# The last row of the first load in a softmax with relative-position bias, loaded by 16 transfers over fewer and fewer partitions

## The chip, the core and the metric

The kernel runs on one core of a Trainium2 chip. The metric is the device time of one execution in microseconds (us). Runs of one kernel on the same chip are compared, with an interval where there are several rounds. The profile is that of one execution; its span runs from the first to the last instruction of the program, and the execution's own time is a little longer than its span.

## What is computed

The inputs are `logits` of shape (2, 8, 2112, 2112) and `rel_bias` of shape (8, 33), both float32. Each head h adds `rel_bias[h, clip(i - j, -16, 16) + 16]` to the logit of query i and key j, and a softmax is taken along the keys:

```
rel = pos[:, None] - pos[None, :]
rel_clipped = np.clip(rel, -max_rel, max_rel) + max_rel
bias = rel_bias[:, rel_clipped].copy()
logits = logits + bias[None, :, :, :]
logits = logits - logits.max(axis=-1, keepdims=True)
exp = np.exp(logits)
return (exp / exp.sum(axis=-1, keepdims=True)).astype(np.float32)
```

Every logit is read once and every result written once: 285.5 MB each way.

## The kernel before

A row is the 2112 logits of one query, 8448 bytes. The 2112 queries of a head are split into 64 blocks of 33 consecutive rows, and the 128 partitions hold the blocks of two heads: partition p has block p mod 64 of head 2k or 2k + 1. The outer index k (4 values, `K`) goes over pairs of heads. For one k there are 12 chunks (`NT`): two batches, and for each the 33 rows of a block in portions of 6, 5, 6, 5, 6 and 5 rows (`SIZES`, L35). So a chunk is 128 partitions times 5 or 6 consecutive rows, and in one transfer each partition moves one contiguous run of 42,240 or 50,688 bytes. There are 48 chunks in all, and 4 buffers `X[0]` to `X[3]` (L44), used in turn.

Four instruction streams work side by side:

- **SyncE (SP)** issues every load and store of chunks, on one queue. `load(k, m)` (L86) brings chunk m into buffer m mod 4 and raises the semaphore `ld` of that buffer by 16. `store(k, m)` (L90) waits until the chunk's rows are scaled, and writes them out. The start (L100) issues the loads of chunks 0 to 3 at once. Then store 0 is issued (L220), and from there `turn` (L214) goes on by a fixed order: store n, wait until store n-1 has landed, load n+3. The last chunk is stored in two parts, three rows and two.
- **VectorE (DVE)** builds, once per k, a strip `F` of biases of width 2144 (`strip`, L143), a shifted window of which is the bias of any row. For each chunk, `add` (L169) takes the buffer's `ld` semaphore and then, row by row, adds the bias and finds the row's extreme (L173). `scale` (L186) takes the sums of the exponentials, forms reciprocals (L189) and scales the first three rows (L193).
- **ScalarE (ACT)** computes the exponentials with their sums (`exps`, L178, L181) and scales the other two or three rows (`scale_rest`, L195, L198). At the start it also issues the small transfer of `rel_bias` over 4 partitions (L107).
- **GpSimd (POOL)** only makes two small index tables at the start (L112). TensorE does nothing.

The order in which the DMA engines see the work of SyncE's queue is thus: load 0, load 1, load 2, load 3, store 0, store 1, load 4, store 2, load 5, and so on. A wait of SyncE for a semaphore is `take` (L82): wait for a count, then subtract it.

The loop of VectorE over k (L202 to L206) calls `strip(k)` and then `add` and `scale` for its 12 chunks; the first chunk of the first k is the one that the change touches.

Of the kernel before, what the change touches and what calls it, by code (L numbers as in the profile page):

```python
# [15 lines left out]
def kernel(  # L16
# [6 lines left out]
    nc = tc.nc  # L23
    P = 128
    B, H, S, S2 = logits.shape
    assert S == S2
    MR = 16
    W = 2 * MR + 1
# [5 lines left out]
    NBUF = 4  # L34
    SIZES = [6, 5, 6, 5, 6, 5]  # L35
# [8 lines left out]
    X = [io.tile([P, R * S], FP32, tag=f"X{b}", name=f"X{b}") for b in range(NBUF)]  # L44
# [11 lines left out]
    def view(t, offset, dims):  # L56
        return bass.AP(tensor=t.tensor, offset=t.offset + offset, ap=[[list(t.ap[0])[0], P]] + dims)

    def rows(t, k, m, s0, n):

        b, j, r = CH[m]
        return bass.AP(
            tensor=t.tensor,
            offset=t.offset + (b * H * S + j + s0) * S + k * (2 * S * S),
            ap=[[W * S, P], [1, n * S]],
        )

    with tc.tile_critical(no_gpsimd_drain=True):  # L68
        ld = [nc.alloc_semaphore(f"ld{b}") for b in range(NBUF)]
        st = [nc.alloc_semaphore(f"st{b}") for b in range(NBUF)]  # L70
        added = nc.alloc_semaphore("added")
        expd = nc.alloc_semaphore("expd")
# [13 lines left out]
        def load(k, m):  # L86
            b, r = m % NBUF, CH[m][2]
            nc.sync.dma_start(out=X[b][:, 0 : r * S], in_=rows(logits, k, m, 0, r)).then_inc(ld[b], 16)
# [8 lines left out]
                out=rows(out, k, m, s0, n), in_=X[b][:, s0 * S : (s0 + n) * S]  # L97
            ).then_inc(st[b], 16)

        for m in range(NBUF):  # L100
            load(0, m)

        Q = 32
        step = list(F.ap[0])[0]
# [3 lines left out]
            out=bass.AP(tensor=F.tensor, offset=F.offset, ap=[[Q * step, P // Q], [1, H * W]]),  # L108
            in_=bass.AP(tensor=rel_bias.tensor, offset=rel_bias.offset, ap=[[0, P // Q], [1, H * W]]),
# [7 lines left out]
        v = nc.vector  # L117
        done = [0]

        def then(ins):  # L120
            done[0] += 1
            ins.then_inc(dve, 1)

        def settle():
            take(v, dve, done[0])
            done[0] = 0
# [9 lines left out]
        for h in range(2):  # L136
            p = slice(h * NB, (h + 1) * NB)
            src = bass.AP(tensor=F.tensor, offset=F[p].offset + h * W,
                          ap=[[list(F.ap[0])[0], NB], [2 * W, K], [1, W]])
# [3 lines left out]
        def strip(k):  # L143

            then(v.tensor_copy(out=rbK[:, :], in_=rbP[:, bass.ds(k, 1), :]))  # L145
            settle()
            low, high = rbK[:, W - 1 : W], rbK[:, 0:1]
            blocks = view(F, MR, [[W, NB], [1, W]])
            then(v.tensor_tensor(out=blocks, in0=view(eq, 0, [[1, NB], [0, W]]),  # L149
                                 in1=view(rbK, W - 1, [[0, NB], [-1, W]]), op=ALU.mult))  # L150
            then(v.tensor_scalar(out=rest, in0=lt, scalar1=low, scalar2=None, op0=ALU.mult))  # L151
            then(v.tensor_copy(out=F[:, 0:MR], in_=low.to_broadcast([P, MR])))  # L152
            then(v.tensor_copy(out=F[:, FW - MR : FW], in_=high.to_broadcast([P, MR])))  # L153
            settle()
            then(v.scalar_tensor_tensor(out=rest, in0=gt, scalar=high, in1=rest, op0=ALU.mult, op1=ALU.add))  # L155
            settle()
            then(v.tensor_tensor(out=blocks, in0=blocks, in1=view(rest, 0, [[1, NB], [0, W]]), op=ALU.add))  # L157
            settle()
# [10 lines left out]
        def add(m):  # L169
            take(v, ld[m % NBUF], 16)  # L170
            j, r = CH[m][1:]
            for i in range(r):
                v.tensor_tensor_reduce(  # L173
                    out=row(m, i), in0=row(m, i), in1=F[:, W - 1 - j - i : W - 1 - j - i + S],
                    scale=-1.0, scalar=BIG, op0=ALU.add, op1=ALU.min, accum_out=col(nmax, m, i),
                ).then_inc(added, 1)
# [9 lines left out]
        def scale(m):  # L186
            r = CH[m][2]
            take(v, expd, r)
            v.reciprocal(out=col(rec, m, 0, r), in_=col(tot, m, 0, r)).then_inc(inv, 1)  # L189
            v.wait_ge(inv, 1).then_inc(inv, -1)  # L190
            v.sem_inc(invA, 1)
            for i in range(DV):
                v.tensor_scalar_mul(out=row(m, i), in0=row(m, i), scalar1=col(rec, m, i)).then_inc(scaled, 1)  # L193
# [7 lines left out]

        with nc.Fori(0, K, 1, engines=[ENG.DVE]) as k:  # L202
            strip(k)
            for m in range(NT):
                add(m)
                scale(m)  # L206
# [54 lines left out]
```

## Time and profile before

| | us |
|---|---|
| median of 3 runs | 1329.67 |
| lowest and highest | 1329.32, 1330.35 |
| the profiled execution | 1329.3 |
| its span | 1327.5 |
| VectorE busy | 819.7 |
| ScalarE busy | 808.8 |

The page of the profile gives first the busy time of each engine and its share of the span; then the span in 40 equal slices, with the mean busy share of the 16 DMA engines in tenths and the GB/s that they moved; then the DMA queues, where q1 is SyncE's and q10 ScalarE's. "Packets" are the pieces that DMA engines moved. A row of the windows view gives a stretch of the span from A to B, its length, the busy time of each compute engine with the number of its instructions, the clock granted to TensorE, the DMA share and the GB/s, where a packet counts in full in the stretch in which it starts. A row of the timeline gives start, length, engine, line, operation, what is written and read, the form, and in brackets the idle time before and what ended it; "SPq" is SyncE's sequencer. A row of a source line gives durations in ns as min/median/max.

### The profile page before, as it was taken

Reading aid. Unit: us, or ns where it says so; the run is one execution under the profiler, and the core shown is the slowest. Engines: PE = TensorE matmul, PEld = TensorE weight load, DVE = VectorE, ACT = ScalarE, POOL = GpSimd, SP = SyncE. Lnnn points to the kernel's source line nnn. Section 1 sums busy time; section 2 is a strip of 40 time slices with the busy share of each in tenths; the row PEclk is TensorE's granted clock in tenths of the full one; section 3 lists DMA queues with packets and bytes.
Section 4 is the critical chain, followed back from the end, with each engine's and each line's share of the span. In section 5 each row is a group of like instructions: output and inputs, shape, how many; then the busy total and the mean of one; then the engine's idle time right before and its main releaser. Section 6 shows DMA issues by size and latency. Waiting matters only on the chain. (4 is left out here: it accounts for less than half of the span.)

```text
span 1327.5 us, 2383 instructions
## 1 busy us (share of the span) xinstructions
DVE 819.7 (62%) x756; ACT 808.8 (61%) x652; POOL 0.6 (0%) x6
## 2 busy tenths in 40 slices
DVE  6875665558655566556866466664686547665572
ACT  3885575655756557555676566764667646675472
POOL 0000000000000000000000000000000000000000
DMA  9999999999999999999999999999999999999998
GB/s 407 427 424 425 430 433 429 432 431 433 434 430 438 423 439 431 432 432 433 438 436 429 433 430 435 433 430 441 427 439 428 435 431 437 434 436 427 436 427 376
DMA packets 13981, 571.00 MB, mean 430 GB/s; under 512 B 1556, under 2 KB 1560, under 8 KB 1560
## 3 DMA queue, kind: packets, MB, share of 16 engines
q1 hardware_dynamic: 13968, 570.96, 99.8%
q14 instruction: 5, 0.04, 0.0%
q10 hardware_dynamic: 8, 0.00, 0.0%
HBM read 285.48 MB, written 285.47 MB: 430 GB/s over the span
## 5 line engine op out<-in xcount | busy, mean ns | idle before, releaser
L173 DVE CUSTOM_DVE_ANT_0 X<-X,F 128x2112 f32<-128x2112 f32 x264 | 605.5, 2354 | 346.8 <-DVEq L83 346.8
L181 ACT ACTIVATE X<-X,nmax 128x2112 f32<-128x2112 f32 x264 | 542.2, 2054 | 411.5 <-ACTq L83 385.7
L198 ACT ACTIVATE X<-X,rec 128x2112 f32<-128x2112 f32 x120 | 238.7, 2046 | 29.0 <-ACTq L83 29.0
L193 DVE TENSOR_SCALAR X<-X,rec 128x2112 f32<-128x2112 f32 x144 | 181.4, 1316 | 11.6 <-DVEq L190 11.6
L189 DVE RECIPROCAL rec<-tot 128x6 f32<-128x6 f32 (+1 forms) x48 | 9.1, 190 | 116.1 <-DVEq L83 116.1
L181 ACT ACTIVATION_READ_ACCUMULATOR X<-X,nmax 128x1 f32 x264 | 49.3, 187 | 0.0
L181 ACT ACT_TABLE_LOAD x4 | 5.1, 1283 | 55.8 <-ACTq L83 55.8
L173 DVE DVE_READ_ACCUMULATOR2_ANT nmax<- 128x1 f32 x264 | 21.7, 82 | 0.0
L157 DVE TENSOR_TENSOR F<-F,rest 128x2112 f32<-128x2112 f32 x4 | 9.4, 2358 | 0.6
L149 DVE TENSOR_TENSOR F<-Z,rbK 128x2112 f32<-128x2112 f32 x4 | 9.4, 2358 | 0.6
L134 DVE LOAD_MASK_SELECT F<-F x1 | 0.0, 14 | 7.1 <-DMA F<-in_rel_bias_dram 7.1
L155 DVE SCALAR_TENSOR_TENSOR rest<-Z,rbK,rest 128x64 f32<-128x64 f32 x4 | 1.1, 284 | 0.6 <-DVEq L83 0.2
L151 DVE TENSOR_SCALAR rest<-Z,rbK 128x64 f32<-128x64 f32 x4 | 1.1, 275 | 0.0
L105 DVE MEMSET F<- 128x264 f32 x1 | 0.3, 278 | 1.1 <-SPq L68 1.1
L145 DVE COPY rbK<-rbP 128x33 f32 x4 | 0.7, 178 | 0.3 <-DVEq L83 0.3
L153 DVE COPY F<-rbK 128x16 f32<-128x16 f32 x4 | 0.7, 168 | 0.0
L152 DVE COPY F<-rbK 128x16 f32<-128x16 f32 x4 | 0.7, 166 | 0.0
L132 DVE TENSOR_SCALAR Z<-F 128x64 f32<-128x64 f32 x3 | 0.5, 223 | 0.1
L140 DVE COPY rbP<-F 64x132 f32<-64x132 f32 x2 | 0.4, 224 | 0.2
L134 DVE STREAM_SHUFFLE F<-F 128x264 f32<-128x264 f32 x1 | 0.4, 443 | 0.0
L112 POOL IOTA F<- 64x64 f32 x2 | 0.4, 179 | 0.7 <-PEq L256 0.6
L245 POOL MEMSET const-bfloat16-1.0<- 128x1 bf16 x1 | 0.1, 103 | 0.0
(3 smaller groups left out, 0.3 us busy)
## 6 DMA issues: line engine op xcount, KB each, us to landing
X<-in_logits_dram SPq DMA_DIRECT2D x24, 6336.0 KB, 39.7
out_dram<-X SPq DMA_DIRECT2D x24, 6336.0 KB, 46.9
X<-in_logits_dram SPq DMA_DIRECT2D x24, 5280.0 KB, 42.2
out_dram<-X SPq DMA_DIRECT2D x23, 5280.0 KB, 48.6
out_dram<-X SPq DMA_DIRECT2D x1, 3168.0 KB, 16.5
out_dram<-X SPq DMA_DIRECT2D x1, 2112.0 KB, 21.1
F<-in_rel_bias_dram ACTq DMA_DIRECT2D x1, 4.1 KB
```

The costliest lines, as they stand in the source:

```text
L145: then(v.tensor_copy(out=rbK[:, :], in_=rbP[:, bass.ds(k, 1), :]))
L149: then(v.tensor_tensor(out=blocks, in0=view(eq, 0, [[1, NB], [0, W]]), in1=view(rbK, W - 1, [[0, NB], [-1, W]]), op=ALU.mult))
L151: then(v.tensor_scalar(out=rest, in0=lt, scalar1=low, scalar2=None, op0=ALU.mult))
L152: then(v.tensor_copy(out=F[:, 0:MR], in_=low.to_broadcast([P, MR])))
L153: then(v.tensor_copy(out=F[:, FW - MR : FW], in_=high.to_broadcast([P, MR])))
L155: then(v.scalar_tensor_tensor(out=rest, in0=gt, scalar=high, in1=rest, op0=ALU.mult, op1=ALU.add))
L157: then(v.tensor_tensor(out=blocks, in0=blocks, in1=view(rest, 0, [[1, NB], [0, W]]), op=ALU.add))
L173: v.tensor_tensor_reduce(out=row(m, i), in0=row(m, i), in1=F[:, W - 1 - j - i : W - 1 - j - i + S], scale=-1.0, scalar=BIG, op0=ALU.add, o ...
L181: nc.scalar.activation(out=row(m, i), in_=row(m, i), func=ACTF.Exp, scale=-1.0, bias=col(nmax, m, i), accum_out=col(tot, m, i),).then_inc( ...
L189: v.reciprocal(out=col(rec, m, 0, r), in_=col(tot, m, 0, r)).then_inc(inv, 1)
L193: v.tensor_scalar_mul(out=row(m, i), in0=row(m, i), scalar1=col(rec, m, i)).then_inc(scaled, 1)
L198: nc.scalar.activation(out=row(m, i), in_=row(m, i), func=ACTF.Copy, scale=col(rec, m, i),).then_inc(scaledA, 1)
```

## The change

The first load, of 6 rows on 128 partitions, is split. Its first 5 rows (`r0`) are loaded by one transfer as before, with the semaphore `ld[0]`. The sixth row of the 128 partitions is loaded by 16 transfers, issued by SyncE between this one and load 1, with a semaphore of their own, `lr`. The first eight, g = 0 to 7, take the partitions g, g + 8, g + 16, ..., over 15 - g partitions. The last eight, g = 7 down to 0, take what is left of each such group, the upper g + 1 partitions. So the numbers of partitions are 15, 14, 13, 12, 11, 10, 9, 8 and then 8, 7, 6, 5, 4, 3, 2, 1: together 128. VectorE waits for `lr` to reach 256, 16 transfers of 16, between `strip(k)` and the first `add`, in each of the four turns of its loop; nothing lowers `lr`, so the wait passes at once after the first turn. Loads 1 to 3 follow in SyncE's queue.

```diff
         ld = [nc.alloc_semaphore(f"ld{b}") for b in range(NBUF)]
+        lr = nc.alloc_semaphore("lr")
...
-        for m in range(NBUF):
+        G = 8
+        N0 = P // G
+        r0 = SIZES[0] - 1
+        nc.sync.dma_start(out=X[0][:, 0 : r0 * S], in_=rows(logits, 0, 0, 0, r0)).then_inc(ld[0], 16)
+
+        def last_row(g, i0, n):
+            p0 = g + G * i0
+            x, d = X[0], rows(logits, 0, 0, r0, 1)
+            step = list(x.ap[0])[0]
+            nc.sync.dma_start(
+                out=bass.AP(tensor=x.tensor, offset=x.offset + p0 * step + r0 * S, ap=[[G * step, n], [1, S]]),
+                in_=bass.AP(tensor=d.tensor, offset=d.offset + p0 * W * S, ap=[[G * W * S, n], [1, S]]),
+            ).then_inc(lr, 16)
+
+        for g in range(G):
+            last_row(g, 0, N0 - 1 - g)
+        for g in reversed(range(G)):
+            last_row(g, N0 - 1 - g, g + 1)
+        for m in range(1, NBUF):
             load(0, m)
...
             strip(k)
+            v.wait_ge(lr, 2 * G * 16)
             for m in range(NT):
```

## The prediction

> **What bounds the kernel.** I read the page first, from its top: who is busy, and in which slices.
>
> ```profile
> span 1327.5 us, 2383 instructions
> DVE 819.7 (62%) x756; ACT 808.8 (61%) x652; POOL 0.6 (0%) x6
> DMA  9999999999999999999999999999999999999998
> DMA packets 13981, 571.00 MB, mean 430 GB/s; under 512 B 1556, under 2 KB 1560, under 8 KB 1560
> q1 hardware_dynamic: 13968, 570.96, 99.8%
> q10 hardware_dynamic: 8, 0.00, 0.0%
> ```
>
> SyncE's queue, q1, occupies the 16 DMA engines for 99.8% of the span, from the second slice to the last but one, while VectorE and ScalarE are idle 38% of it. So the time is the bytes over the rate, plus what an engine loses at the ends and in between. The bytes don't change here; only rate and ends can.
>
> The same lines tell how a transfer is dealt out. There are 97 transfers of 128 partitions (48 loads, 49 stores) and one of 4 partitions, rel_bias on q10. The packets under 512 B are 1556 = 97 x 16 + 4, and q10 has 8 packets, 4 of them data: each engine that takes part adds one small closing packet, a full transfer runs on 16 engines, and the one of 4 partitions ran on 4. So I expect a transfer of n rows on n below 16 partitions to run on n engines, one row each.
>
> Next the rate in stretches of 100 us; the last two columns are the DMA share and GB/s.
>
> ```profile
> core 0: us, DVE busy (x) ACT busy (x) POOL busy (x), PEclk, DMA share, GB/s
> 0.00:100.00 100.00, 73.29 (x75) 67.90 (x55) 0.56 (x6) 1.00 1.00 421
> 100.00:200.00 100.00, 62.40 (x56) 61.52 (x51) 0.00 (x0) 1.00 0.99 427
> 200.00:300.00 100.00, 56.52 (x51) 58.04 (x46) 0.00 (x0) 1.00 1.00 432
> 300.00:400.00 100.00, 68.67 (x66) 64.20 (x54) 0.00 (x0) 1.00 1.00 432
> 400.00:500.00 100.00, 59.05 (x53) 58.18 (x46) 0.00 (x0) 1.00 1.01 434
> ...
> 700.00:800.00 100.00, 59.12 (x54) 58.10 (x48) 0.00 (x0) 1.00 1.00 430
> 800.00:900.00 100.00, 59.29 (x54) 62.82 (x50) 0.00 (x0) 1.00 1.00 434
> ...
> 1200.00:1300.00 100.00, 62.40 (x56) 62.74 (x51) 0.00 (x0) 1.00 1.00 430
> ```
>
> There is a flat ceiling of 434 GB/s, 27.1 per engine, and the rate climbs to it over 400 us: the engines are busy throughout, but their packets last longer at first. Against 434, the first four stretches lose 13, 7, 2 and 2 GB/s, which is 3.0 + 1.6 + 0.5 + 0.5 = 5.6 us. Of that 2.0 us is the start, as the next rows show.
>
> ```profile
> 0.00:2.00 2.00, 0.76 (x4) 0.00 (x0) 0.56 (x6) 1.00 0.26 76
> 2.00:4.00 2.00, 0.00 (x0) 0.00 (x0) 0.00 (x0) 1.00 1.08 329
> ```
>
> Packets start only toward 2 us, and the first of them run at 329: (1 - 329/434) x 2, so 0.5 us and somewhat more, say 0.9 us, is ramp. That leaves **2.7 us of early loss**. The other two slow stretches lose 0.9 us each. Then the end, us by us.
>
> ```profile
> 1321.00:1322.00 1.00, 0.00 (x0) 0.00 (x0) 0.00 (x0) 1.00 0.87 372
> 1322.00:1323.00 1.00, 0.00 (x0) 0.00 (x0) 0.00 (x0) 1.00 0.75 321
> 1323.00:1324.00 1.00, 0.00 (x0) 0.00 (x0) 0.00 (x0) 1.00 0.47 203
> 1324.00:1325.00 1.00, 0.00 (x0) 0.00 (x0) 0.00 (x0) 1.00 0.28 118
> 1325.00:1326.00 1.00, 0.00 (x0) 0.00 (x0) 0.00 (x0) 1.00 0.12 51
> 1326.00:1327.50 1.50, 0.00 (x0) 0.00 (x0) 0.00 (x0) 1.00 0.00 0
> ```
>
> All engines have the same bytes, yet they finish over some 4 us. From 1322 on 321 + 203 + 118 + 51 = 693 KB are left, which 16 engines together would move in 693/434 = 1.6 us: the mean engine ends near 1323.6, the last near 1326.0. **The last engine is 2.4 us behind the mean.** Then 1.5 us to the end of the span, and 1.8 us outside it: 1329.3 for this execution. The median of the runs, 1329.67, is 0.4 above; I work in the former and add 0.4 at the end.
>
> My reading of both: the engines start side by side, and all change from load to store at once; packets there are slow. The delays differ by engine and push them apart; once they are some 4 us apart the rate stays at 434. The change sets them apart from the start.
>
> **The change part by part.**
>
> Bytes and packets: 128 rows of 8448 B leave the first load and return as 16 transfers. One row at an engine's rate is 8448 B / 27.1 GB/s = 0.31 us. The first load was 6 x 8 rows an engine and becomes 5 x 8. If a transfer over n partitions always uses the same first n engines, the first engine gets a row from each of the 16 transfers, the next from 15, and so on; the eighth 9, the ninth 7, the last none. The mean stays 8. The spread is 16 x 0.31 = 5.0 us, and the first engine has 8 x 0.31 = 2.5 us more than the mean. Nothing returns that: the queue never runs dry, so **the engine that is made late is late at the end.** Of the closing packets there are 128 more, 16 on the first engine; their price lies inside the 0.31 per row up to a few ns (bounds 0 and 0.1 us in all).
>
> Issue: SyncE must issue 17 transfers where it issued one before load 1.
>
> ```profile
> L88 SPq DMA_DIRECT2D X<-in_logits_dram x48: 339/349/512, 1.0 to 1244.0; - x48
> L107 ACTq DMA_DIRECT2D F<-in_rel_bias_dram x1: 1098/1098/1098, 1.4 to 1.4; - x1
> 0.97 1.88 SPq L88 DMA_DIRECT2D X<-in_logits_dram  x4
> ```
>
> The first four issues took 1.88 us, 0.47 each; the one issue over few partitions, on another engine's queue, took 1.10. Bounds for 16: 5.6 (0.35 each) to 17.6 us; I take 0.47, by SyncE's own rows: 7.5 us, and load 1 goes out at 1.0 + 0.5 + 7.5 = 9.0. What hides it is the five-row load: 40 x 0.31 = 12.4 us from about 2 us plus 0.9 of ramp, until 15.3. At 1.10 each load 1 is issued at 19.1 and the early engines stand idle for some 4 us; the first engine does not, as its own rows last beyond 20.3.
>
> The new wait: VectorE waits for all 16 transfers ahead of the first row, and what is queued behind it is every row pass, and behind these ScalarE and store 0.
>
> ```profile
> 18.60 2.36 DVE L173 CUSTOM_DVE_ANT_0 X<-X,F 128x2112 f32<-128x2112 f32 x1 [2.15 <-DVEq L83]
> 41.38 16.61 SPq L96 DMA_DIRECT2D out_dram<-X  x2
> ```
>
> Row pass one starts at 18.60 now. With the last row landing between 20.3 and 28 it slips by up to 10 us, and store 0 from 41.4 to at most 52. Loads 1 to 3 (16 rows x 8 x 0.31 = 39.7 us) hold the earliest engine until 15.3 + 39.7 = 55. So it costs nothing; without that cover, early engines would lose their lead, and the late one nothing. In later rounds the count is already reached, and the wait is free.
>
> Stalls: of the 2.7 us of early loss I take 2.0 away (bounds: 0, if standing apart is not the cause, and 4.5, if the two slow stretches go too). The old lag of 2.4 us goes as well, because the planned order takes its place.
>
> The price of a row is the open term. [...] I take 0.62 for the first eight and 0.78, the middle, for the last eight: 5.0 + 6.2 = 11.2 us, because the rate that repeats in loads and stores points to the side that both pass. Against the old 2.5 that is **+8.7**.
>
> [...]
>
> Sum: -2.4 (old lag) - 2.0 (early loss) + 8.7 = +4.3 on 1329.3, so 1333.6, and on the median's scale **1334.0**.
>
> **The rivals.**
>
> Rows at full speed: the first engine's rows take 5.0, +2.5. Then -2.4 - 2.0 + 2.5 = -1.9, 1327.8 on the median's scale; with all 2.7 and the slow stretches gone, down to 1325.3; I take 1327.0. [...]
>
> Standing apart doesn't cure the early loss (or slow issues undo it), at full-speed rows: -2.4 + 2.5 = +0.1, plus the chance lag of up to 2.4 on the first engine: 1329.8 to 1332.2, or slower yet if the late engine stalls more than the mean. For it: a stretch at 430 comes back at 700 and at 1200 us, long after the engines parted.
>
> It doesn't do what it says: short transfers start on changing engines, so that each gets about 8 rows. Then the lag and early loss stay: 1329.7 to 1330. The counts above say how many engines take part, not which. [...]
>
> The forecast ends on the slower side and the first rival on the other; what decides is the first engine's time for 16 rows. At 6.9 us the time is that of before.
>
> **How the numbers follow.** About 0.2%, 2.7 us, is what a measurement tells from no change: under 1327.0 is faster, over 1332.3 slower. Forecast 0.45 (own range 1332 to 1336: slower 0.41, same 0.04). Rows at full speed 0.36 (faster 0.22, same 0.14). No cure 0.13 (same 0.06, slower 0.07). Even deal 0.06 (same). Together 0.22, 0.30, 0.48. The range of 8 in 10 reaches from the full-speed rival, 1326.0, to 1335.8, short of three-way sharing with no cure.
>
> **What would show it.** Packets under 512 B: 1556 + 128 = 1684 if n rows take n engines. The rate in the first 400 us near 434 if the cure holds. At the end, a tail that starts earlier and lasts 10 us or more with sharing, about 5 without. VectorE's first row pass at 26 to 28 us with sharing, near 21 without. Load 1's issue at 9.0. The sum fails if the late engine is not the first one, if the queue runs dry, or if it falls further behind at every change from load to store.

## The result, and the profile after

The changed kernel takes **1334.24 us**, the median of 7 runs (1334.00 to 1334.51); the kernel before takes 1329.63 beside it. The ratio is 1.0035, with a 95% interval of 1.0023 to 1.0047: slower by some 4.6 us. The profiled execution took 1334.34 with a span of 1332.6 us.

The page of the changed kernel, the lines that answer to those shown of before:

```profile
span 1332.6 us, 2399 instructions
DVE 819.7 (62%) x756; ACT 808.8 (61%) x652; POOL 0.6 (0%) x6
DMA  9999999999999999999999999999999999999997
DMA packets 14237, 571.00 MB, mean 428 GB/s; under 512 B 1684, under 2 KB 1688, under 8 KB 1688
q1 hardware_dynamic: 14224, 570.96, 99.5%
```

The busy times and the bytes are those of before, and the small packets are the 1684 that were forecast: a transfer over n partitions ran on n engines. Then the rate in stretches, the last column being GB/s:

```profile
0.00:100.00 100.00, 69.51 (x72) 63.89 (x53) 0.56 (x6) 1.00 0.99 400
100.00:200.00 100.00, 63.41 (x56) 62.37 (x49) 0.00 (x0) 1.00 1.00 434
200.00:300.00 100.00, 57.67 (x54) 61.20 (x50) 0.00 (x0) 1.00 1.00 433
300.00:400.00 100.00, 67.96 (x64) 61.95 (x52) 0.00 (x0) 1.00 1.00 434
...
700.00:800.00 100.00, 58.67 (x53) 57.71 (x45) 0.00 (x0) 1.00 1.00 432
...
1200.00:1300.00 100.00, 59.38 (x53) 58.12 (x47) 0.00 (x0) 1.00 1.00 433
```

Two things changed in opposite directions. From 100 us on the kernel is better than before, which had 427, 432 and 432 in the next three stretches and 430 at 700 and 1200 us. The first 100 us are far worse, 400 in place of 421. Where, the finer stretches show:

```profile
4.00:15.00 11.00, 6.04 (x11) 0.00 (x0) 0.00 (x0) 1.00 1.00 430
15.00:16.00 1.00, 0.38 (x1) 0.00 (x0) 0.00 (x0) 1.00 0.74 254
16.00:18.00 2.00, 0.00 (x0) 0.00 (x0) 0.00 (x0) 1.00 1.24 262
18.00:20.00 2.00, 0.00 (x0) 0.00 (x0) 0.00 (x0) 1.00 1.40 275
20.00:22.00 2.00, 0.00 (x0) 0.00 (x0) 0.00 (x0) 1.00 1.11 194
22.00:24.00 2.00, 0.00 (x0) 0.00 (x0) 0.00 (x0) 1.00 0.96 211
24.00:26.00 2.00, 0.00 (x0) 0.00 (x0) 0.00 (x0) 1.00 0.65 211
26.00:28.00 2.00, 1.01 (x1) 0.00 (x0) 0.00 (x0) 1.00 1.08 465
```

From 15 to 26 us, while the 16 narrow transfers run, the engines have packets under way (the share is 0.65 to 1.40) and move 194 to 275 GB/s, about half of the 430 of the stretch before. From 15 to 28 us they moved 254 + 2 x (262 + 275 + 194 + 211 + 211 + 465) = 3490 KB, which at 434 would take 8.0 us and not 13: by these rows 5.0 us lost on the mean engine.

Two things about such sums. A packet counts in full where it starts, and 16 packets of 50,688 bytes that start together are 0.81 MB. So while the engines stand side by side, the edge of a stretch of 100 us can move its rate by up to 8 GB/s. The trace also keeps every packet of the DMA engines with start, duration and size, but without its engine; numbers from there are marked "by the packet records". With the bytes of each packet spread over its duration, and against 433.8 GB/s, the most that any stretch of 100 us reached so, the loss from 15 to 28 us is **5.5 us on the mean engine**: 2.2 in the narrow rows, 3.1 in the first packets of load 1, the rest in closing packets. Within one engine a packet starts 3 or 4 ns before its predecessor ends: where one is alone at the end, packets of 629 ns start 625 or 626 apart. So the packets can mostly be strung into 16 chains, one for each engine. In the kernels with a staircase the engines are numbered here by the narrow rows in their chains, the first having most.

The timeline has the issues and the end of the rows:

```profile
1.40 11.78 SPq L110 DMA_DIRECT2D X<-in_logits_dram  x16
13.23 1.30 SPq L89 DMA_DIRECT2D X<-in_logits_dram  x3
26.99 2.36 DVE L192 CUSTOM_DVE_ANT_0 X<-X,F 128x2112 f32<-128x2112 f32 x1 [11.61 <-DVEq L84]
```

And the end:

```profile
1322.00:1324.00 2.00, 0.00 (x0) 0.00 (x0) 0.00 (x0) 1.00 0.89 380
1324.00:1326.00 2.00, 0.00 (x0) 0.00 (x0) 0.00 (x0) 1.00 0.53 228
1326.00:1328.00 2.00, 0.00 (x0) 0.00 (x0) 0.00 (x0) 1.00 0.18 76
1328.00:1330.00 2.00, 0.00 (x0) 0.00 (x0) 0.00 (x0) 1.00 0.06 25
1330.00:1332.60 2.60, 0.00 (x0) 0.00 (x0) 0.00 (x0) 1.00 0.02 6
```

An engine moves 42,240 bytes in 1.561 us, 27 GB/s, so after 1328, at 25 GB/s, a single engine is still at work. The packet records put the end of the last engine at 1331.0, of the one before it at 1327.9 and of the mean engine at 1325.6. Before, these were 1326.1, 1325.8 and 1323.8.

### The profile page after: what moved, and what is told of

The parts are those of the page before. It is cut to its first block, busy times and chain, and to the rows that moved or that the text cites. A ratio compares the mean times of both kernels' runs of the same rounds, so it can differ in the third digit from the quotient of the medians.

```text
span 1332.6 us, 2399 instructions
## 1 busy us (share of the span) xinstructions
DVE 819.7 (62%) x756; ACT 808.8 (61%) x652; POOL 0.6 (0%) x6
## 2 busy tenths in 40 slices
DMA packets 14237, 571.00 MB, mean 428 GB/s; under 512 B 1684, under 2 KB 1688, under 8 KB 1688
```

## The experiments

The theory, called S, is that engines which write certain sets of partitions at the same time hold one another up, and that this is what the narrow transfers cost. It is called sharing below; the runs can show its price for a set, not how it comes about. Its rivals: O, small transfers with their closing packets are slow by themselves; H, reading HBM at rows 8 blocks apart is slow. Beside this stand two questions of the prediction: does standing apart cure the early loss, and is an engine that is made late at the start late at the end? All ratios are against the kernel before, run beside. Edits are shown against the kernel before unless the text says otherwise, and `...` marks lines left out; VectorE's wait for `lr` is for 16 times the number of narrow transfers each time. "Rows" are packets of one row, 8448 bytes; their times are from the packet records, as are the ends of engines.

**The row as one transfer.** By none of the three theories should this cost anything. Each experiment of the first kind has the five-row load of the changed kernel and brings the sixth row by other transfers. Here `last_row` takes the first partition, the step between partitions and their number; the next kernels differ from this one only in the calls shown.

```diff
-        for m in range(NBUF):
+        r0 = SIZES[0] - 1
+        nc.sync.dma_start(out=X[0][:, 0 : r0 * S], in_=rows(logits, 0, 0, 0, r0)).then_inc(ld[0], 16)
+
+        def last_row(p0, d, n):
...
+                out=bass.AP(tensor=x.tensor, offset=x.offset + p0 * step + r0 * S, ap=[[d * step, n], [1, S]]),
+                in_=bass.AP(tensor=t.tensor, offset=t.offset + p0 * W * S, ap=[[d * W * S, n], [1, S]]),
...
+        last_row(0, 1, P)
+        for m in range(1, NBUF):
             load(0, m)
```

> [...] Rival O (rows in small pieces are slow by themselves, because of the closing packets or short packets): one closing packet for eight rows, so no loss either. Rival H (the slow thing is reading HBM at rows 8 blocks apart): no loss. This is the control.

Measured: 1329.83, ratio 1.0001 (0.9991 to 1.0011); all 128 packets of 8448 B took 0.319 us. Splitting the load off costs nothing.

**Sixteen partitions, 8 apart.**

```diff
+        for g in range(8):
+            last_row(g, 8, 16)
```

> The last row by eight transfers over 16 partitions that lie 8 apart: every engine gets eight rows with eight closing packets, none is made late. Theory S: two engines meet everywhere, a row takes 0.62 us, every engine loses 8 x 0.31 = 2.5 us, time about 2.5 us above before, 1332. Rivals O and H: rows of 0.62 us as well, the same time. Between 16 and 26 us the changed kernel moved 194 to 275 GB/s; here some 5 us at 220.

Measured: 1331.46, ratio 1.0013 (1.0004 to 1.0023). The rate, and VectorE's first row pass (18.60 before):

```profile
15.00:18.00 3.00, 0.46 (x1) 0.00 (x0) 0.00 (x0) 1.00 0.96 239
18.00:21.00 3.00, 0.00 (x0) 0.00 (x0) 0.00 (x0) 1.00 1.21 346
```

```profile
21.21 2.36 DVE L187 CUSTOM_DVE_ANT_0 X<-X,F 128x2112 f32<-128x2112 f32 x1 [5.75 <-DVEq L84]
```

The median row takes 0.62 us, nearly twice 0.319, though every engine has an even share. By itself this fits all three.

**Sixteen neighbours**, with the same number of transfers and packets.

```diff
+        for g in range(8):
+            last_row(16 * g, 1, 16)
```

> As with partitions 8 apart, but each of the eight transfers takes 16 neighbouring partitions. Number of transfers, packets and closing packets is the same. [...] Rival O: rows as with partitions 8 apart, same time as there. Rival H: the rows read lie closer together in HBM, so rows are faster than there, time 1330 to 1332.

Measured: 1334.74, ratio 1.0037 (1.0025 to 1.0050).

```profile
15.00:18.00 3.00, 0.56 (x1) 0.00 (x0) 0.00 (x0) 1.00 1.03 175
18.00:21.00 3.00, 0.00 (x0) 0.00 (x0) 0.00 (x0) 1.00 1.01 149
```

Slower than 8 apart with all else equal: O and H both fall on this, since the number of packets is the same and the rows read lie closer. Rows had a median of 0.89 us, against 0.62 with 8 apart.

**Neighbours in another order** bears on that; the edit is against the kernel just shown.

```diff
-        for g in range(8):
+        for g in (0, 2, 1, 3, 4, 6, 5, 7):
             last_row(16 * g, 1, 16)
```

> The eight transfers over 16 neighbouring partitions in another order: 0, 32, 16, 48, 64, 96, 80, 112. [...] If 0.89 is a limit of its own, rows and time stay at 0.83 on average and 1334.7.

Measured: 1336.03, ratio 1.0049 (1.0033 to 1.0064).

```profile
15.00:18.00 3.00, 0.60 (x1) 0.00 (x0) 0.00 (x0) 1.00 1.01 149
18.00:21.00 3.00, 0.00 (x0) 0.00 (x0) 0.00 (x0) 1.00 1.09 132
```

The same eight transfers, only in another order, are 1.3 us slower; their rows took 0.99 us on the mean (0.83 before) and up to 1.31. So 0.89 is no limit of its own: the order of the sets counts too. Why, no run tells.

**Sixteen partitions, 7 apart.**

```diff
+        for g in range(7):
+            last_row(g, 7, 16)
+        last_row(112, 1, 16)
```

> The last row by seven transfers over 16 partitions 7 apart (0 to 111) and one over the neighbours 112 to 127; eight rows and eight closing packets per engine, as with 8 apart (1331.5, rows of 0.62 us) and with neighbours (1334.7, rows of 0.89 us). [...]

Measured: 1331.13, ratio 1.0011 (1.0001 to 1.0020). Rows had a median of 0.41 us against 0.62 with a step of 8. The time is only 0.3 us below that of 8 apart: the mean engine ended at 1324.3 (1326.0 with 8 apart), but the last engine 3.6 behind it, where in the kernel before it was 2.3. Why the field was wider here no run tells; in the six kernels that give every engine an even share it was 2.0 to 3.6, one execution each.

**The changed kernel with neighbouring rows of HBM.** The edit is against the changed kernel.

```diff
-                in_=bass.AP(tensor=d.tensor, offset=d.offset + p0 * W * S, ap=[[G * W * S, n], [1, S]]),
+                in_=bass.AP(tensor=d.tensor, offset=d.offset + p0 * W * S, ap=[[S, n], [1, S]]),
```

> The changed kernel with one difference: the 16 transfers read neighbouring rows of HBM (each transfer n consecutive rows of one block) and not rows 8 blocks apart. The sixth row of chunk 0 is thus filled with other rows of the logits, and its results are those of other rows. The partitions written are the same. Theory S and rival O: the same as the changed kernel, 1334.2, rows of 0.6 to 0.9 us. Rival H: rows of 0.32 us, time 1327 to 1329.

Measured: 1333.88, ratio 1.0032 (1.0020 to 1.0043); rows 0.58 us on the mean, 0.60 in the changed kernel. The rate dips as in the changed kernel, which had 259 and 239 in these two stretches:

```profile
15.00:18.00 3.00, 0.42 (x1) 0.00 (x0) 0.00 (x0) 1.00 1.09 268
18.00:21.00 3.00, 0.00 (x0) 0.00 (x0) 0.00 (x0) 1.00 1.30 251
```

H is out.

**One engine made late, without sharing.** Sixteen one-row transfers behind load 0, each over one partition, go into columns of the buffers that nothing reads.

```diff
+        load(0, 0)
...
+        y, t = X[1], rows(logits, 0, 0, 0, 1)
...
+        for i in range(16):
+            p = (0, 1, 2, 3, 32, 33, 34, 35)[i % 8]
+            if i == 8:
+                y = X[3]
+            nc.sync.dma_start(
+                out=bass.AP(tensor=y.tensor, offset=y.offset + p * step + 5 * S, ap=[[step, 1], [1, S]]),
+                in_=bass.AP(tensor=t.tensor, offset=t.offset + p * W * S, ap=[[W * S, 1], [1, S]]),
+            ).then_inc(lr, 16)
```

> [...] The output is unchanged; 135 KB more are moved, all by one engine. If the engine that is made late at the start is late at the end, the time is that of the mean engine before plus 16 x 0.325 = 5.2 us, less the old lag: 1329.6 - 2.4 + 5.2 = 1332.4, up to 2.4 more if that engine has a chance lag too. If lateness is absorbed by the queue or by slack in the chain, 1329.6. The early loss of 2.7 us should stay, since 15 of the 16 engines still start together.

Measured: 1330.18, ratio 1.0004 (0.9994 to 1.0013), 2.2 us less than forecast. All 16 rows took 0.319 us, one behind the other on one engine. At the end the last engine is alone, at 1326.9, 1.7 behind the next and 5.7 behind the earliest (1321.2). The field of the kernel before was 4.2 us wide without any late engine, so this alone would not show who is last. The chains do: the engine with the 16 rows was 5.3 us behind the earliest at 45 us, 5.9 at 100 and 5.8 at 600. So the lateness of 5.2 us was kept; my miss was to count it from the mean engine. It adds to the end of the earliest engines, because the late one takes less of the early loss (from 30 to 400 us 2.7 us, the others 1.8 to 5.4); and most of it stands where the ordinary lag stood.

**A staircase without sharing.**

```diff
+        load(0, 0)
...
+        t = rows(logits, 0, 0, 0, 1)
+        for i in range(16):
+            y = X[1 if i < 8 else 3]
+            step = list(y.ap[0])[0]
+            p = (0, 1, 2, 3, 32, 33, 34, 35)[i % 8]
+            n = 8 - i // 2
+            nc.sync.dma_start(
+                out=bass.AP(tensor=y.tensor, offset=y.offset + p * step + 5 * S, ap=[[4 * step, n], [1, S]]),
+                in_=bass.AP(tensor=t.tensor, offset=t.offset + p * W * S, ap=[[4 * W * S, n], [1, S]]),
+            ).then_inc(lr, 16)
```

> A staircase without sharing: the kernel before, with 16 more transfers behind load 0, over 8, 8, 7, 7, ... 1, 1 partitions 4 apart, into a part of the buffers that nothing reads. [...] 0.6 MB more are moved. Rows should take 0.32 us, if sharing is all that made them slow. [...] In the staircases so far one engine of the late group, not the last of it at the start, fell back by 2.5 to 4 us during the run and ended 2 to 3 us behind the next. If that engine is one of the first eight and falls back by itself, it ends alone here too, and the time is 1330.5 to 1332; if it fell back because of the sharing at the start, the time is 1329.5 to 1330.5.

Measured: 1331.10, ratio 1.0009 (1.0000 to 1.0018).

```profile
15.00:18.00 3.00, 1.55 (x1) 0.00 (x0) 0.00 (x0) 1.00 0.93 400
18.00:21.00 3.00, 0.00 (x0) 0.00 (x0) 0.00 (x0) 1.00 1.03 439
21.00:24.00 3.00, 0.12 (x1) 0.00 (x0) 0.00 (x0) 1.00 0.95 408
```

Each of the 72 rows took 0.319 us, with 16 narrow transfers, 72 closing packets and up to 8 engines at once: **with these partitions the rate does not dip.** It is 400 to 439 where 16 partitions 8 apart had 239 and 346. O is out a second time. The last engine ended at 1327.3, the next at 1326.9: nobody was alone. By the ends of the engines the question about the engine that falls back stays open; the chains answer it. The fifth engine, with 8 rows, was 2.6 us behind the earliest at 45 us, 4.3 at 400 and 5.8 at 900. From 100 us on it is the one whose full packets, some 25 in every 100 us, last 1 to 12 ns longer, and the chain that carries these ends last. The first engine was at 5.7, 6.4 and 6.9. So the fifth fell back by itself, without sharing; it had started so far ahead of the first that it passed it only at the end.

**A staircase 7 apart.**

```diff
+        for r in range(7):
+            last_row(r, 7, 15 - 2 * r)
+        for r in reversed(range(7)):
+            last_row(r + 7 * (15 - 2 * r), 7, 1 + 2 * r)
+        last_row(112, 1, 16)
```

> The staircase of the changed kernel with partitions 7 apart: transfers over 15, 13, 11, ... 3 partitions, then 1, 3, ... 13 over what is left of each sixteen, and one over 112 to 127. The first engine gets 15 rows, the last one 1. [...] If sharing makes the loss and the planned spread cures the early loss (100 to 400 us at 433 or 434 GB/s), the time is 1331 to 1332, or 1329 where no engine falls back later. If the time stays at 1334, sharing is not the price.

Measured: 1332.95, ratio 1.0026 (1.0016 to 1.0035).

```profile
0.00:100.00 100.00, 71.06 (x74) 65.42 (x54) 0.56 (x6) 1.00 0.99 405
100.00:200.00 100.00, 63.37 (x57) 62.22 (x51) 0.00 (x0) 1.00 1.01 434
200.00:300.00 100.00, 56.17 (x53) 59.79 (x48) 0.00 (x0) 1.00 1.00 433
300.00:400.00 100.00, 69.13 (x65) 63.06 (x53) 0.00 (x0) 1.00 1.00 434
```

The early loss is nearly as absent as in the changed kernel, and from 15 to 28 us the mean engine lost 4.1 us in place of 5.5 by the packet records. The time is 1.3 us below that of the changed kernel, as less sharing would have it, and a little above the forecast, since again one engine ended alone, at 1329.7, 3.0 us behind the next.

**The dose.** In three kernels the 16 transfers bring only the last columns of the row, and the first `c0` columns come with the five rows: 1584 for a quarter, 1056 for half, 528 for three quarters. The edit is against the changed kernel, here for a quarter.

```diff
-        nc.sync.dma_start(out=X[0][:, 0 : r0 * S], in_=rows(logits, 0, 0, 0, r0)).then_inc(ld[0], 16)
+        c0 = 1584
...
+            out=X[0][:, 0 : r0 * S + c0],
...
-                out=bass.AP(tensor=x.tensor, offset=x.offset + p0 * step + r0 * S, ap=[[G * step, n], [1, S]]),
-                in_=bass.AP(tensor=d.tensor, offset=d.offset + p0 * W * S, ap=[[G * W * S, n], [1, S]]),
+                out=bass.AP(tensor=x.tensor, offset=x.offset + p0 * step + r0 * S + c0, ap=[[G * step, n], [1, S - c0]]),
+                in_=bass.AP(tensor=d.tensor, offset=d.offset + p0 * W * S + c0, ap=[[G * W * S, n], [1, S - c0]]),
```

> A quarter of the dose: the last 528 columns of each row come by the 16 transfers. Spread at the start 2.5 to 3 us, sharing costs the mean engine 1.3 us. If the cure holds at that spread, 1327.3 to 1329, faster than before; if not, 1329.5 to 1331.

> The changed kernel with half the dose: the 16 transfers bring only the second half of each row, 1056 columns; the first half comes with the five rows. Rows of half length: sharing and planned spread are both half, the loss by sharing some 2.5 us in place of 5.1 on the mean engine, the spread at the start 5 in place of 10 us. If the early loss is cured by a spread of 4 us and more, the time is 1330 to 1331.5; if the cure needs the full spread, 1332 or more.

> Three quarters of the dose: the last 1584 columns of each row come by the 16 transfers. With the full dose 100 to 400 us ran at 433 or 434 GB/s, with half at 430 to 433. Sharing costs three quarters, 3.8 us on the mean engine. If the cure grows with the spread, the early loss lies between, and the time is 1333 to 1334; if half a dose had all the cure that there is, the time lies on the line from half (1332.3) to full (1334.2), 1333.2, with 430 to 433 GB/s.

Measured: 1331.44 (ratio 1.0013, 1.0003 to 1.0022), 1332.30 (1.0018, 1.0009 to 1.0027) and 1332.91 (1.0023, 1.0014 to 1.0032). No dose is faster than before. The rate shows the early loss still there; here the quarter dose and half the dose:

```profile
100.00:200.00 100.00, 62.41 (x56) 61.36 (x51) 0.00 (x0) 1.00 1.00 429
200.00:300.00 100.00, 56.13 (x51) 58.20 (x46) 0.00 (x0) 1.00 1.00 430
300.00:400.00 100.00, 69.16 (x66) 64.29 (x54) 0.00 (x0) 1.00 1.00 432
```

```profile
100.00:200.00 100.00, 62.10 (x55) 60.70 (x49) 0.00 (x0) 1.00 1.00 430
200.00:300.00 100.00, 55.85 (x53) 58.86 (x48) 0.00 (x0) 1.00 1.00 432
300.00:400.00 100.00, 69.15 (x66) 63.69 (x53) 0.00 (x0) 1.00 1.00 433
```

The table has, by the packet records, how far the last engine stood behind the earliest at 45 us, when the start is over; what the mean engine lost against 433.8 GB/s from 100 to 400 us and from 28 to 1300 us; and the ends of the engines. Each row is one execution.

```
kernel                      spread  lost, 100-400, 28-1300   last, next, mean engine
before                      0.4     1.8  4.5                 1326.1 1325.8 1323.8
8 apart, even               0.4     1.8  4.4                 1328.2 1328.1 1326.0
one engine late             5.3     1.8  3.6                 1326.9 1325.2 1323.2
quarter                     1.9     1.6  3.3                 1328.5 1325.6 1323.6
half                        2.6     1.7  3.4                 1328.9 1326.9 1324.9
three quarters              3.6     0.7  2.7                 1329.6 1328.1 1326.2
without sharing, 8 engines  5.7     0.3  2.3                 1327.3 1326.9 1323.0
7 apart                     4.9     0.4  1.5                 1329.7 1326.7 1324.9
full, neighbouring rows     4.8     0.5  0.9                 1330.5 1327.7 1325.4
full                        4.8     0.3  0.8                 1331.0 1327.9 1325.6
```

In the kernel with one late engine the other 15 stood within 0.6 us. The kernels that give every engine an even share lost from 3.2 to 4.9 us from 28 to 1300 us, so the quarter and half the dose can't be told from no cure; three quarters and more can, from 100 to 400 us above all. Half the dose gave a spread of 2.6 us, not the 5 that I had expected, and so was no test of a spread of 4. The cure thus came with spreads of 3.6 us and more; with lateness of one engine, or with sharing without a staircase, 1.8 us were lost from 100 to 400 us, as before.

## Why the prediction was right, and what in it was not

The forecast was 1334.0, the result 1334.24, slower as forecast. The steps one by one:

**Deal and packets: right.** 1684 small packets; n rows on n engines.

**The price of a row: right in kind and nearly in size.** The sum has 0.62 us a row and then 0.78, twice and two and a half times 0.31. That was my estimate of engines that hold one another up, two or three at a time; no run shows these terms. What the changed kernel showed in their place, by the packet records: the first row of each engine took 0.319 us, rows from 16 to 20.4 us took 0.55 to 0.70, later ones up to 0.91, and the last ones 0.54 to 0.59. The last row ended at 25.8 us, the first began at 15.2: 10.6 us where I took 11.2, or +8.1 for +8.7. VectorE's first row pass came at 26.99, within the 26 to 28. The rival of rows at full speed fell here. Loads and stores do run at one rate, as the sum has it: in the kernel before 42,240 B took 1.561 us at the median from 2 to 45 us, in loads alone, and from 1290 to 1330 us, in stores alone. Which side limits it no run shows. The experiments rank the sets of partitions: rows took 0.319 us in one transfer over 128 partitions, over one partition at a time, and 4 apart over at most 8; 0.41 at the median for 7 apart and 0.62 for 8 apart; with neighbours 0.83 and 0.99 on the mean in two orders, and 1.31 at most. Why they rank so no run tells.

**I did not count what the engines in load 1 pay.** While narrow rows were still being written, an engine in load 1 needed up to 3.9 us for a packet of 42,240 B that otherwise takes 1.56. These packets are 3.1 of the 5.5 us that the mean engine lost, and the reason why the spread by load 3 was only 4.8 us by the packet records, not the 11 of the first engine's rows. It didn't change the sum, which follows the late engines.

**The early loss: right in kind, too small in size.** I took 2.0 us away. By the packet records the mean engine lost 4.5 us from 28 to 1300 us before and 0.8 after: 1.2 were saved up to 100 us, 1.5 from 100 to 400 us and 1.1 later, with rounding 3.7 in all. (What I had read off the stretches as 2.7 up to 400 us and 1.8 later is 3.1 and 1.4 by these records.) One execution can differ from another by some 0.8 here. The rival that standing apart cures nothing fell.

**The old lag of 2.4 us: this step failed.** I let it go, as the planned order would take its place. The planned order came, and another lag on top of it: one engine ended 3.1 us behind the next, and it was not the first one, which the prediction had named as a sign that the sum fails. With the measured terms, -2.4 - 3.7 + 8.1 = +2.0, the time by my steps would be 1331.3; the second-last engine's end, 1327.9, with 1.6 to the end of the span and 1.8 outside, makes 1331.3 too. The last engine adds 3.1: 1334.4, and the profiled execution took 1334.34. That the forecast came out so closely is luck: a gain that I made 1.7 too small and rows that I made 0.6 too dear stood against a lag that I left out.

The chains show whose lag that is. In each of the ten kernels that were strung so, one engine has packets that often last 1 to 12 ns longer, and where narrow rows name the engines (the changed kernel, the one with neighbouring rows, the staircase without sharing) it is the fifth, as far as the chains hold. In the changed kernel its packets took 3.0 us more from 400 us on than the usual 1.561 and 1.872; of the other engines none lost more than 0.8. In the kernel before and in the one with a late engine, where it starts level with the others, it ended in the middle of the field. The staircase over 15 engines puts it fifth from the end at the start, so that it falls through to the last place. Why its packets last longer no run tells.

**Issue: the price was wrong, the cover held.** The 16 issues took 11.78 us, 0.74 each, for my 0.47; load 1 went out at 13.23, not 9.0. The five-row load kept the engines busy until 15.2, so nothing ran dry. **The wait** cost nothing, as said: store 0 was issued at 49.8, and load 3 held even the earliest engine until 61.

The bargain behind the change is thus real, with both sides measured: 3.7 us of early loss saved on the mean engine, against 5.5 us lost to sharing there. The mean engine ended 1.8 us later, and the last engine 5.3 behind it, where before it was 2.3. Without sharing (72 rows at 0.319) it still did not pay, 1331.1; but that kernel moves 0.6 MB more, 1.4 us on the mean engine, so it does not price a staircase that moves no more bytes. No run tried one without sharing.

## What to carry to other kernels

Here the DMA engines were busy for more than 99% of the span, and the end belonged to the engine that was latest; one that got 5.2 us more at the start was 5.3 us behind the earliest at 45 us and 5.7 at the end. What the time paid for it depended on how far the engines drifted apart anyway: 5.2 us given to one engine cost 0.4, within the noise, while in the staircases the late start of the fifth engine added to a lag of its own. A row in a transfer over few partitions took from 0.319 to 0.99 us on average here, by where the partitions lay: compare the rate of the stretch in which such a transfer runs with that of the full transfers, here 434 GB/s. And a gain and its price may come in one edit, here 3.7 us and 5.5 on the mean engine: split the span into stretches, or a result near zero will look like no effect. When the engines move in step, mind the edges of the stretches, worth up to 8 GB/s here.

## What the runs showed of the hardware that was not expected

What a narrow transfer cost SyncE to issue went by its form: in the changed kernel 425 to 1009 ns with a median of 710, against 339 to 512 for loads over 128 partitions. The lines are those of the changed kernel, of 16 partitions 8 apart, of 16 neighbours, and of the one-row transfers over one partition, which are the cheapest:

```profile
L110 SPq DMA_DIRECT2D X<-in_logits_dram x16: 425/710/1009, 1.4 to 12.8; - x16
L107 SPq DMA_DIRECT2D X<-in_logits_dram x8: 589/590/849, 1.4 to 6.1; - x8
L107 SPq DMA_DIRECT2D X<-in_logits_dram x8: 402/426/445, 1.4 to 4.7; - x8
L108 SPq DMA_DIRECT2D X<-in_logits_dram x16: 232/266/516, 1.4 to 6.4; - x16
```

In the kernel before, the sixteen engines stood within 0.4 us of one another at 45 us, and lost 1.4 us each from 28 to 100 us, 1.8 from 100 to 400 and 1.3 in the 900 us after that. In the five staircases with a spread of 3.6 us or more, 0.3 to 0.7 were lost from 100 to 400 us. The prediction read the cause as the change from load to store that all make at once. The packet records bear this out and name the place: in the kernel before, loads 3 to 8, each followed by a store in the queue, lost 2.0 us on the mean engine in their last two packets, 0.8 of it in load 3. Loads 1 and 2, which are followed by a load, lost 0.03 together. In the changed kernel the same six loads lost 0.03. Why the last packets of such a load are slow no run tells.
